# Second head's z in seven block products, with the fourth block sum made earlier

## The chip, the core and the metric

The kernel runs on one core of one Trainium2 chip. The metric is the device time of one execution in microseconds (us), median of several runs. The profile shows the core's engines: TensorE (PE, matmuls; PEld its weight loads), VectorE (DVE), ScalarE (ACT), GpSimd (POOL), and the queue of SyncE (SP), which issues most DMAs.

## What is computed

A decoder trunk of two layers over x of 1024 tokens by 1024 channels in float32: a gated DeltaNet layer (GDN), then an mLSTM layer, then a norm. The change is in the GDN layer alone:

```
h = rmsnorm(x, norm_w[i])
p = h @ w_in                                  # q, k, v, z, a, bt of 8 heads
q, k, v = silu(causal_dwconv(qkv))            # q, k: 128 wide a head, v: 256
q, k = l2norm(q) * HEAD_QK ** -0.5, l2norm(k)
# per head, by chunks: S_t = exp(g_t)(I - beta_t k_t k_t^T) S_{t-1} + beta_t k_t v_t^T;  o_t = S_t^T q_t
o = gated_delta_chunked(q, k, v, g, beta)
o = rmsnorm(o, norm_w) * silu(z)
x = x + o @ w_out
```

z of a head is 256 columns of h @ w_in.

## The kernel before

**Precision.** Each operand of the large products is split in a high and a low part (`hi` and `lo`, L280 on ScalarE and L281 on GpSimd or, for some, VectorE), and each product takes three matmuls: hi by hi, hi by lo, lo by hi.

**Blocks.** h is cut in four blocks A11, A12, A21, A22 (first index the half of the tokens, second the half of the channels). From them come the sums S1 to S4, made once for the whole layer: S1 = A21 + A22, S3 = A21 - A11, S2 = S1 - A11 by `h_blocks` (L486, L488, L489 on VectorE, split by L468 on ScalarE and L469), four channel blocks one after the other; S4 = A12 - S2 by `last_block` (L473, L477, L478 on VectorE, split by L468 and L469). S4 is put where A21's tiles were. A pair of column blocks of the weights can then be multiplied in two ways. `Columns` takes the blocks as they are: eight products. `Pair` takes seven (in the manner of Strassen and Winograd) and needs S1 to S4, sums of weights (L596, L597, L603, L604) and sums of results (L626, L631, L637, L643, L651, all on VectorE), and seven split operands where `Columns` splits four. One product (`product`, L511) is twelve matmuls of 128x512. In before heads 0 and 1 have their z by `Columns`, all later heads by `Pair`.

**Order.** TensorE's order is written by hand. Three matmuls of `product` are a step; `plan` names for each step the generators that run a bit there: `gdn_scan` (the chunks of a head's scan), `gdn_keys`, `gdn_queries`, `gdn_solve`, `gdn_merge`, `gdn_tokens`, `first_blocks`, `last_block`. The numbers are in the tables KEYS, QUERIES, SOLVE, MERGE, TOKENS, SCAN (one entry each for head 0, head 1 and all later heads, counted from the head's base), BLOCKS and LAST. A base is the number of steps of the heads before: 64 for the first, 96 for the second, 88 for each later one. A scheduler sets the order on the other engines from the order in which the code runs and from its estimates, so that a table's number moves instructions there too.

**The scan.** A chunk c of head h is `ks` (TensorE, state by key, L1061), `rr` (VectorE, L1063), `y` (TensorE, L1066), `w` (ScalarE, L1068), `sn` and `o` (TensorE, L1073, L1082, L1083), the new state S (VectorE, L1078; L1076 for the first chunk), then the gate and its transposes `go` (L386, L383). Each waits for the one ahead. Chunks are numbered 0 to 7: y0_7 is the last `y` of head 0. While head 0 is scanned, head 1's columns are multiplied (gkv1, gvq1, gz1, named `gkv_ps`, `gvq_ps`, `gzp_ps` in the trace), its keys prepared (`tpk` L886, `kk` L928, `nt` L931, two halves: kk1_0 and kk1_1), its triangular system solved on VectorE (L977, L979, 31 rounds) and merged (`xp`, `yl`, L1016; the solution goes through DRAM as `tb` and comes back as `td`, copied by L1006 and transposed by L1002).

Of the kernel before, what the change touches and what calls it, by code (L numbers as in the profile page):

```python
# [17 lines left out]
P = 128  # L18
# [23 lines left out]
OUT0 = "k", "wraw"  # L42
VT = ("ccpx", "ccpb")

F0STEPS = 6, 16
R8 = range(8)
LOOK = 2
VLO = (((1, 3, 6, 7), (1, 2, 3, 5, 7)), ((3, 6, 7), (1, 3, 5, 7)))
# [6 lines left out]
LASTENDS = ((4, 4), (6, 8), (8, 8))  # L55


KEYS = ((4, 9, 10, 17), (26, 29, 30, 33), (22, 25, 26, 29))
QUERIES = ((20, 22, 25, 32), (68, 71, 76, 76), (80, 80, 84, 89))
SOLVE = (24, 41, 38)  # L60
MERGE = (78, 97, 89)
TOKENS = ((37, 37, 81, 85), (74, 77, 100, 106), (64, 74, 103, 109))
SCAN = (95, 110, 102)
PACE = ((3, 3, 8), (4, 3, 10), (4, 3, 11))
BLOCKS = (106, 115, 114, 126)
XLOADS = (24, 116)
LAST = (158, 148, 156, 164)
TH = HT * P


# [1 line left out]
def hybrid_kernel(ctx, tc, x_in, norm_w, final_norm_w, gdn_w_in, gdn_conv_w, gdn_a_log, gdn_dt_bias, gdn_norm_w,  # L72
# [422 lines left out]
    def last_block(temp, e):  # L495

        for k in range(4):
            a = temp(k)
            whole(V, a, blocks["A12"][k])
            add_parts(V, a, a, blocks["S2"][k], ALU.subtract)  # L500
            put("S4", k, a, e)
            yield
# [202 lines left out]
    def out_heads(half, heads, gs, name):  # L705

        for jj in range(0, KT // 2, 2):
            pss = [pwork(f"{name}{half}_{jj}{i}", "ppbx"[i]) for i in range(4)]
            for h in heads:
                for j in range(2):  # L710
                    hi, lo = operand()
                    for i in range(2):
                        for e in range(ET):
                            ghi, glo = gs[h, e]
                            for m, (a, b) in enumerate(((hi, ghi), (hi, glo), (lo, ghi))):
                                mm(pss[2 * j + i], a[:, e, i * P:(i + 1) * P], b, start=h == heads[0] and e == 0 and m == 0,  # L716
                                   stop=h == heads[-1] and e == ET - 1 and m == 2)
                            if (i, e) != (1, ET - 1):
                                yield
                    if h == heads[-1]:  # L720
                        for i in range(2 * j, 2 * j + 2):
                            V.tensor_tensor(x[2 * jj + i][half], x[2 * jj + i][half], pss[i], ALU.add)
                    yield
# [27 lines left out]
    def do(gen, n=1):  # L751
        for _ in range(n):
            next(gen, None)
# [100 lines left out]
    def gdn_z(h, st):  # L854
        st["gate"] = [None, None]

        def sink(e, half, src):
            if st["gate"][half] is None:
                st["gate"][half] = hp.tile([P, ET, TH], F32, tag="gate", bufs=GB, name=f"gz{h}_{half}")
            A.activation(st["gate"][half][:, e, :], src, AF.Silu)  # L860

        c0 = 2 * QK + DI + h * DV
        if h < 2:
            return Columns(gdn_w_in, c0, c0 + P, f"gzp{h}", sink, small=h == 0)
        return Pair(gdn_w_in, c0, c0 + P, f"gzp{h}", sink, in_psum=(True, False), bank="b")

    def gdn_tokens(h, st):

        for half in range(2):
            v = hp.tile([P, HT, DV], F32, tag="v", bufs=2, name=f"gv{h}_h{half}")  # L870
            st["v"].append(v)
            for e in range(ET):
                vp = pwork(f"gvp{h}_{e}_{half}", "d")
                for c in range(HT):
                    nc.tensor.transpose(vp[:, c * P:(c + 1) * P], st["vt"][e, half][:, c * P:(c + 1) * P], ident)
                A.copy(v[:, :, e * P:(e + 1) * P], vp.rearrange("p (c d) -> p c d", c=HT))
                if e == ET - 1:
                    G.tensor_tensor(v, v, st["irk"][:, half * HT:half * HT + HT].unsqueeze(2).to_broadcast([P, HT, DV]),
                                    ALU.mult)
                yield  # L880
# [62 lines left out]
    def gdn_queries(h, st):  # L943

        sq, eq = (sp.tile([P, NT], F32, tag=n, name=f"{n}{h}") for n in ("sq", "eq"))
        st["eq"] = eq
        for half in range(2):
            hs = slice(half * HT, half * HT + HT)
            q, k, at = st["q"][half], st["k"][half], st["at"][half]
            squares_t(q, sq, "q", h, half)  # L950
            V.tensor_scalar(eq[:, hs], sq[:, hs], 1e-6, EPS * DK, ALU.add, ALU.mult)
            dec_b = decay_row(1, h, half)
            yield
            kq = pwork(f"kq{h}_{half}", "d").rearrange("p (c i) -> p c i", c=HT)
            for c in range(HT):
                s_ = slice(c * P, (c + 1) * P)
                mm(kq[:, c, :], k[:, s_], q[:, s_], start=True, stop=True)
            V.tensor_tensor(at, kq, at, ALU.mult)
            G.tensor_tensor(q, q, dec_b, ALU.mult)
            yield  # L960

    def gdn_solve(h, st):


        nd = st["nd"].rearrange("p (j i) -> p j i", i=BLK)
        rows = sp.tile([P, BLK // NG4 * BLK], F32, tag="t", bufs=2, name=f"xr{h}")
        nc.sync.dma_start(rows, unit_rows)
        xp = pwork(f"xt{h}", "x")[:, :BLK // NG4 * BLK] if h > 1 else rows
        xt = xp.rearrange("p (i r) -> p i r", r=BLK)
        if h > 1:  # L970
            A.copy(xp, rows)
        yield
        for j in range(BLK - 1):
            m, n = j // NG4 + 1, BLK - 1 - j
            pr = sp.tile([P, m, n], F32, tag="td", bufs=1, name=f"pr{h}_{j}")
            with behind() if j == 0 else nullcontext():
                V.tensor_tensor(pr, xt[:, :m, j:j + 1].to_broadcast([P, m, n]),  # L977
                                nd[:, j:j + 1, j + 1:].to_broadcast([P, m, n]), ALU.mult)
            st["solved"] = V.tensor_tensor(xt[:, :m, j + 1:], xt[:, :m, j + 1:], pr, ALU.add)  # L979
            yield  # L980
        st["tb"] = dp.tile([NG4, NT, NB, BLK // NG4, BLK], F32, tag="tb", bufs=2, name=f"tb_dram{h}")
        if h > 1:
            A.copy(rows, xp)
        nc.sync.dma_start(st["tb"].rearrange("g c b i r -> (g c b) (i r)"), rows)
        st["td"] = tds = sp.tile([P, NT, BLK], F32, tag="td", bufs=1, name=f"td{h}")
        for g in range(NG4):
            nc.sync.dma_start(tds[g::NG4], st["tb"][g].rearrange("c b i r -> (b i) c r"))
        yield
# [124 lines left out]
    with tc.manual_schedule(engines={mybir.EngineType.PE}):  # L1113
        sts = [{} for _ in range(H)]
        diags = []
        cols = [c for h in range(H) for c in (*gdn_columns(h, sts[h]), gdn_z(h, sts[h]))]
        gs = [{}, {}]
        parts0 = g_parts(gg_dram, range(H - 1), 0, gg_place(0), "gl", gs[0])
# [21 lines left out]
        def at_steps(steps, gen):  # L1140
            for step in steps:
                plan.setdefault(step, []).append(gen)

        base, starts = 0, []
        for h in range(H):
            starts.append(base)
            base += (64, 96)[h] if h < 2 else 88
        end = base
        for h, (st, base) in enumerate(zip(sts, starts)):
            i = min(h, 2)  # L1150
            b, (l, m, p) = SCAN[i] + base, PACE[i]
            scan = [b, b + m]
            for c in range(1, NT):
                c0 = b + m + p - l - m + p * (c - 1)
# [3 lines left out]
        for h, (st, base) in enumerate(zip(sts, starts)):  # L1158
            i = min(h, 2)
            off = lambda steps: [base + n for n in steps]  # L1160
            at_steps(off(range(MERGE[i] - 4, MERGE[i] + 16, 4)), gdn_merge(h, st))
            at_steps(off(KEYS[i]), gdn_keys(h, st, range(2)))
            at_steps(off(QUERIES[i]), gdn_queries(h, st))
            at_steps(off(SOLVE[i] + n // 2 for n in range(BLK + 1)), gdn_solve(h, st))
            at_steps(off(TOKENS[i]), gdn_tokens(h, st))
        temps = lambda k: [wp.tile([P, TH], F32, tag="wraw", bufs=WB, name=f"hs{k}_{i}") for i in range(2)]

        def first_blocks():
            gen = h_blocks(temps, (G, V, G))
            for k in range(4):  # L1170
                with tc.issue_after(sts[0]["merged" if k else "solved"].ins):
                    next(gen)
                yield

        at_steps(BLOCKS, first_blocks())
        at_steps(LAST, last_block(lambda k: temps(k)[0], V))

# [430 lines left out]
    with tc.manual_schedule(engines={mybir.EngineType.PE}):  # L1608
# [5 lines left out]
        for n, _ in enumerate(out_heads(1, heads, gss[1], "lout")):  # L1614
            if n == F0STEPS[0]:
                do(f0)
            if n >= F0STEPS[1] and n % 2 == 0:
                do(f0)
# [61 lines left out]
```

## Time and profile before

| | us |
|---|---|
| median of three runs | 1923.8 (1923.57 to 1925.78) |
| the profiled execution | 1924.86 |
| its span | 1923.1 |
| TensorE busy | 1872.0 (97%), 9764 matmuls |
| VectorE busy | 1256.2 (65%) |
| ScalarE busy | 1016.1 (53%) |
| GpSimd busy | 701.4 (36%) |

The page gives the busy time of each engine, the span in slices, and the costliest groups. Matmuls overlap, so their busy times add up to more than the time they take; the distance from one start to the next is what one costs. The list of waits gives, for an engine, who ended its idle time; the timeline gives single instructions with start, duration and, in brackets, the idle time ahead of them.

### The profile page before, as it was taken

What the parts mean: (1) busy time and instruction counts of PE and PEld (TensorE: products, weight loads), DVE (VectorE), ACT (ScalarE), POOL (GpSimd) and SP (SyncE); (2) the same over time, 40 slices, a digit from 0 to 9 for tenths busy, and PEclk for the clock granted to TensorE, in tenths of its full rate; (3) what the DMA queues carried; (4) which work ended last, traced back from release to release, by engine and by line L of the source; (5) the groups of instructions that cost most, each with busy time, mean ns of one, the idle gap of its engine ahead of it and who ended that gap; (6) DMA issues with size and microseconds to landing.
All of it is one profiled execution on the core that took longest, in us unless ns stands there. A gap on an engine that the chain in (4) does not pass through costs nothing. (4 is left out here: it accounts for less than half of the span.)

```text
span 1923.1 us, 28886 instructions
## 1 busy us (share of the span) xinstructions
PE 1872.0 (97%) x9764; PEld 1545.2 (80%) x9764; DVE 1256.2 (65%) x2856; ACT 1016.1 (53%) x2336; POOL 701.4 (36%) x662
## 2 busy tenths in 40 slices
PE   5999999999999999999999999999999999999998
PEld 3777888888888887788878888888888888878886
DVE  7579686859585858548566866666666666673413
ACT  5555565655556555545346454555454555574523
POOL 4234334343433434101031433333333333345553
PEclk9999999999999999999999999999999999999999
DMA  4211122222222222646322221212121222245342
GB/s 144 92 48 55 48 72 80 62 77 66 68 78 64 79 59 90 198 130 215 121 71 73 66 77 56 79 58 83 61 83 61 72 69 66 77 140 181 131 137 72
DMA packets 138621, 171.25 MB, mean 89 GB/s; under 512 B 30860, under 2 KB 68584, under 8 KB 138472
## 3 DMA queue, kind: packets, MB, share of 16 engines
q1 hardware_dynamic: 137896, 168.87, 28.0%
q8 instruction: 77, 1.26, 0.3%
q14 instruction: 72, 0.59, 0.1%
q10 hardware_dynamic: 576, 0.52, 0.1%
HBM read 142.87 MB, written 26.48 MB: 88 GB/s over the span
## 5 line engine op out<-in xcount | busy, mean ns | idle before, releaser
L425 POOL TENSOR_TENSOR g_r<-g_r,mhalf 128x1 f32<-128x1 f32 x64 | 40.3, 629 | 195.3 <-DVE g_r L424 194.6
L286 DVE SCALAR_TENSOR_TENSOR gw_lo<-gw_raw,rest,gw_hi 128x256 fp32r<-128x256 f32 x128 | 64.1, 539 | 63.8 <-ACT gw_hi L285 63.6
L281 POOL TENSOR_TENSOR lw_lo<-lw_raw,lw_hi 128x512 fp32r<-128x512 f32 x56 | 72.4, 1296 | 73.8 <-ACT lw_hi L280 67.9
L281 POOL TENSOR_TENSOR mz_lo<-mz_raw,mz_hi 128x512 fp32r<-128x512 f32 x40 | 53.7, 1342 | 102.9 <-ACT mz_hi L280 102.7
L285 ACT ACTIVATE gw_hi<-gw_raw,rest 128x256 fp32r<-128x256 f32 x128 | 58.0, 501 | 61.8 <-PE gout L716 34.1
L716 PE MATMUL lout<-lgp_hh,lw_hi 128*128 128x512 f32 x224 | 88.6, 395 | 0.9 <-DVE mg L1371 0.9
L281 POOL TENSOR_TENSOR mog_lo<-mog_raw,mog_hi 128x512 fp32r<-128x512 f32 x39 | 51.4, 1319 | 104.1 <-ACT mog_hi L280 104.1
L716 PE MATMUL lout<-lgp_hh,lw_lo 128*128 128x512 f32 x224 | 87.3, 390 | 0.0
L716 PE MATMUL lout<-lgp_hl,lw_hi 128*128 128x512 f32 x224 | 87.2, 389 | 0.0
L281 POOL TENSOR_TENSOR mv_lo<-mv_raw,mv_hi 128x512 fp32r<-128x512 f32 x38 | 51.9, 1366 | 83.2 <-ACT mv_hi L280 50.6
L511 PE MATMUL gkv_ps<-hh,gkv_hi 128*128 128x512 f32 x176 | 77.6, 441 | 0.0
L280 ACT CAST lw_hi<-lw_raw 128x512 fp32r<-128x512 f32 x56 | 34.6, 620 | 79.2 <-PE lout L716 41.1
L281 POOL TENSOR_TENSOR gzp_lo<-gzp_raw,gzp_hi 128x512 fp32r<-128x512 f32 x38 | 50.0, 1317 | 67.6 <-ACT gzp_hi L280 53.9
L281 POOL TENSOR_TENSOR gkv_lo<-gkv_raw,gkv_hi 128x512 fp32r<-128x512 f32 x40 | 52.2, 1304 | 61.6 <-ACT gkv_hi L280 56.0
L281 POOL TENSOR_TENSOR mkq_lo<-mkq_raw,mkq_hi 128x512 fp32r<-128x512 f32 x35 | 45.1, 1289 | 75.2 <-ACT mkq_hi L280 61.8
L511 PE MATMUL gkv_ps<-hh,gkv_lo 128*128 128x512 f32 x176 | 69.4, 394 | 0.0
L511 PE MATMUL gkv_ps<-hl,gkv_hi 128*128 128x512 f32 x176 | 69.0, 392 | 0.0
L716 PE MATMUL gout<-glp_hh,gw_hi 128*128 128x512 f32 x160 | 66.5, 415 | 0.0
L425 POOL TENSOR_TENSOR m_r<-m_r,mhalf 128x1 f32<-128x1 f32 x64 | 42.9, 671 | 59.4 <-DVE m_r L424 52.6
L281 POOL TENSOR_TENSOR gqv_lo<-gqv_raw,gqv_hi 128x512 fp32r<-128x512 f32 x30 | 40.4, 1345 | 64.1 <-PE sn L1073 27.1
L716 PE MATMUL gout<-glp_hh,gw_lo 128*128 128x512 f32 x160 | 62.7, 392 | 0.0
L716 PE MATMUL gout<-glp_hl,gw_hi 128*128 128x512 f32 x160 | 62.4, 390 | 0.0
(765 smaller groups left out, 6653.2 us busy)
## 6 DMA issues: line engine op xcount, KB each, us to landing
gw_raw<-in_gdn_w_out_dram SPq DMA_DIRECT2D x64, 256.0 KB, 2.8
lw_raw<-in_mlstm_w_out_dram SPq DMA_DIRECT2D x56, 256.0 KB, 2.8
gzp_raw<-in_gdn_w_in_dram SPq DMA_DIRECT2D x32, 256.0 KB, 3.2
growb<-g_dram SPq DMA_DIRECT2D x32, 256.0 KB, 3.3
gg_dram<-gv_h SPq DMA_DIRECT2D x64, 128.0 KB, 1.8
gl<-gg_dram SPq DMA_DIRECT2D x32, 256.0 KB, 3.4
mog_raw<-in_mlstm_w_in_dram SPq DMA_DIRECT2D x32, 256.0 KB, 3.1
mz_raw<-in_mlstm_w_in_dram SPq DMA_DIRECT2D x32, 256.0 KB, 3.0
```

The source lines that it names most:

```text
L280: A.copy(hi, raw)
L281: (e or G).tensor_tensor(lo, raw, hi.bitcast(F32), ALU.subtract)
L285: A.activation(hi[:, k], raw[:, k], AF.Copy, scale=c)
L286: V.scalar_tensor_tensor(lo[:, k], raw[:, k], c, hi.bitcast(F32)[:, k], ALU.mult, ALU.subtract)
L425: G.tensor_tensor(r, r, mhalf[:, :1], ALU.pow)
L511: mm(ps, w_[:, k, :], h_, start=first and k == 0 and i == 0, stop=k == 3 and i == 2, skip_group_check=True)
L716: mm(pss[2 * j + i], a[:, e, i * P:(i + 1) * P], b, start=h == heads[0] and e == 0 and m == 0, stop=h == heads[-1] and e == ET - 1 and m == 2)
```

## The change

Head 1's z becomes a `Pair`, as the later heads' is, and only head 0 keeps `Columns`. Its 32 steps become 28, so the second head's length is 92 and all later bases are four sooner. S4 must now be there for head 1's z (steps 148 to 151) and not first for head 2: LAST goes from steps 148 to 164 to steps 123 to 142. BLOCKS, the scan of head 0 (two steps sooner), the second half of head 1's keys (three later), its queries and solve (four later), and the queries and solve of the later heads get other steps.

```diff
-KEYS = ((4, 9, 10, 17), (26, 29, 30, 33), (22, 25, 26, 29))
-QUERIES = ((20, 22, 25, 32), (68, 71, 76, 76), (80, 80, 84, 89))
-SOLVE = (24, 41, 38)
+KEYS = ((4, 9, 10, 17), (26, 29, 30, 36), (22, 25, 26, 29))
+QUERIES = ((20, 22, 25, 32), (72, 75, 80, 80), (78, 78, 83, 87))
+SOLVE = (32, 45, 29)
...
-SCAN = (95, 110, 102)
+SCAN = (93, 110, 102)
...
-BLOCKS = (106, 115, 114, 126)
+BLOCKS = (98, 119, 111, 123)
...
-LAST = (158, 148, 156, 164)
+LAST = (123, 130, 136, 142)
...
         c0 = 2 * QK + DI + h * DV
-        if h < 2:
-            return Columns(gdn_w_in, c0, c0 + P, f"gzp{h}", sink, small=h == 0)
+        if h == 0:
+            return Columns(gdn_w_in, c0, c0 + P, f"gzp{h}", sink, small=True)
         return Pair(gdn_w_in, c0, c0 + P, f"gzp{h}", sink, in_psum=(True, False), bank="b")
...
-            base += (64, 96)[h] if h < 2 else 88
+            base += (64, 92)[h] if h < 2 else 88
```

On TensorE, in the second head's first stretch of gvq1, there stands before, from the second half of the keys (kk1_1) over the first chunk's `sn` and `o`:

```order
L928 MATMUL kk1_1_1521<-gkT1_1_1280 128x128 x4
L511 MATMUL gvq1_ps00_1504<-hh0_2_0_243,gvq1_00_hi_1295 128x512
L511 MATMUL gvq1_ps00_1504<-hl0_2_0_244,gvq1_00_hi_1295 128x512
L511 MATMUL gvq1_ps00_1504<-hh0_2_0_243,gvq1_00_lo_1296 128x512
L1073 MATMUL sn0_0_1543<-w0_0_1502,kd0_668 128x256
L1083 MATMUL o0_0_1547<-w0_0_1502,at0_0_682 128x256
```

and a little further on, from `ks` of chunk 1, in after:

```order
L1061 MATMUL ks0_1_1531<-S0_0_1515,gkT0_0_368 128x256
L511 MATMUL gvq1_ps00_1504<-hh0_3_0_248,gvq1_00_hi_1295 128x512
L511 MATMUL gvq1_ps00_1504<-hl0_3_0_249,gvq1_00_hi_1295 128x512
L511 MATMUL gvq1_ps00_1504<-hh0_3_0_248,gvq1_00_lo_1296 128x512
L511 MATMUL gvq1_ps01_1505<-hh0_0_1_408,gvq1_00_hi_1295 128x512
L511 MATMUL gvq1_ps01_1505<-hl0_0_1_409,gvq1_00_hi_1295 128x512
L511 MATMUL gvq1_ps01_1505<-hh0_0_1_408,gvq1_00_lo_1296 128x512
L928 MATMUL kk1_1_1563<-gkT1_1_1280 128x128 x4
```

So kk1_1 stood ahead of `sn` and `o` of chunk 0 and now stands behind `ks` of chunk 1.

On VectorE at the same place (L931 is nt of the keys' first half, L486 to L489 and L469 the block sums, L326 a convolution) there stands before:

```order
L931 SCALAR_TENSOR_TENSOR nt1_0_1454<-kk1_0_1449,nb1_1404,at1_0_1420 128x128 x4
L326 SCALAR_TENSOR_TENSOR gvT1_0_1_1493<-gkv1_ps11_1288,gcw_159,gvT1_0_1_1493 128x511
L486 TENSOR_TENSOR hs2_1_1790<-x2_1_80,x6_1_88 128x512
L469 TENSOR_TENSOR S2hl1_1777<-hs1_1_1764,S2hh1_1776 128x512
L910 TENSOR_TENSOR kd1_1406<-tpk1_1_1471,ekd_277 128x512
L920 TENSOR_SCALAR sk1_1401<-sk1_1401 128x4
L326 SCALAR_TENSOR_TENSOR gvT1_0_1_1493<-gkv1_ps11_1288,gcw_159,gvT1_0_1_1493 128x510
L488 TENSOR_TENSOR hs2_0_1789<-x2_1_80,x2_0_79 128x512
L1076 COPY S0_0_1545<-sn0_0_1543 128x256
```

and now:

```order
L931 SCALAR_TENSOR_TENSOR nt1_0_1458<-kk1_0_1453,nb1_1404,at1_0_1420 128x128 x4
L486 TENSOR_TENSOR hs2_1_1810<-x2_1_80,x6_1_88 128x512
L1076 COPY S0_0_1515<-sn0_0_1513 128x256
L326 SCALAR_TENSOR_TENSOR gvT1_0_1_1497<-gkv1_ps11_1288,gcw_159,gvT1_0_1_1497 128x511
L469 TENSOR_TENSOR S2hl1_1696<-hs1_1_1683,S2hh1_1695 128x512
L910 TENSOR_TENSOR kd1_1406<-tpk1_1_1475,ekd_277 128x512
```

The first state S0_0, which ks0_1 needs, comes six rows nearer to L931.

On VectorE at the end of head 0's scan (rr0_7 is what y0_7 needs; S4hl, hs and the S2 tiles belong to S4) there stands before:

```order
L1063 SCALAR_TENSOR_TENSOR rr0_7_2167<-ks0_7_2165,nlam_276,gv0_h1_1305 128x256
L1002 STREAM_TRANSPOSE nd1_1405<-td1_1868 32x8x32 x3
L469 TENSOR_TENSOR S4hl0_2175<-hs0_0_2169,S4hh0_2174 128x512
L469 TENSOR_TENSOR S4hl1_2231<-hs1_0_2225,S4hh1_2230 128x512
L473 TENSOR_TENSOR hs2_0_2252<-hh0_6_0_263,hl0_6_0_264 128x512
L473 TENSOR_TENSOR hs3_0_2318<-hh0_7_0_268,hl0_7_0_269 128x512
L477 TENSOR_TENSOR hs2_0_2252<-hs2_0_2252,S2hh2_1802 128x512
```

and now:

```order
L977 TENSOR_TENSOR pr1_28_1896<-xr1_1652,nd1_1405 128x24
L1063 SCALAR_TENSOR_TENSOR rr0_7_2206<-ks0_7_2204,nlam_276,gv0_h1_1305 128x256
L979 TENSOR_TENSOR xr1_1652<-xr1_1652,pr1_28_1896 128x8x3
L637 TENSOR_TENSOR gzp1_u4_2113<-gzp1_u4_2113,gzp1_ps7_2152 128x512
L977 TENSOR_TENSOR pr1_29_1928<-xr1_1652,nd1_1405 128x16
L979 TENSOR_TENSOR xr1_1652<-xr1_1652,pr1_29_1928 128x8x2
L977 TENSOR_TENSOR pr1_30_1931<-xr1_1652,nd1_1405 128x8
L979 TENSOR_TENSOR xr1_1652<-xr1_1652,pr1_30_1931 128x8
L643 TENSOR_TENSOR gzp1_ps5_2114<-gzp1_u2_1961,gzp1_ps5_2114 128x512
```

S4's work stands ahead of rr0_7 now, and the end of the second head's solve (L977, L979) has come behind it.

## Rows read from the trace of the kernel before

**Rows 1.** The page, first part: busy time, share of the span and instructions.

```profile
PE 1872.0 (97%) x9764; PEld 1545.2 (80%) x9764; DVE 1256.2 (65%) x2856; ACT 1016.1 (53%) x2336; POOL 701.4 (36%) x662
```

**Rows 2.** Windows: length, then busy us (instructions) of each engine, clock, DMA.

```profile
140.00:180.00 40.00, 35.44 (x171) 28.35 (x170) 36.00 (x72) 22.52 (x59) 19.52 (x16) 0.96 0.17 50
```

**Rows 3.** Waits of TensorE, 140 to 260 us: total, times, longest.

```profile
PE kk L928 <- DVE nt L931: 2.8, 1, 2.8
PE y L1066 <- DVE rr L1063: 0.9, 1, 0.9
PE ks L1061 <- DVE S L1078: 0.4, 1, 0.4
PE yl L1016 <- ACT nd L1033: 0.4, 1, 0.4
PE gvp L875 <- ACT sqrq L889: 0.3, 1, 0.3
```

**Rows 4.** Timeline, TensorE: start, duration, instruction, [idle before it and its releaser].

```profile
145.79 1.05 PE L928 MATMUL kk<-gkT 128*128 128x128 f32 x8
...
153.35 1.53 PE L928 MATMUL kk<-gkT 128*128 128x128 f32 x8 [2.85 <-DVE nt L931]
...
215.03 0.59 PE L1066 MATMUL y<-rr,nt 128*128 128x256 f32 x2
...
223.88 0.69 PE L1016 MATMUL xp<-nd,nt 32*32 32x32 f32 x32
```

**Rows 5.** Windows, TensorE alone: length, busy (instructions), granted clock, DMA.

```profile
153.97:157.39 3.42, 3.42 (x13) 0.50 0.58 173
```

**Rows 6.** Timeline, VectorE, from 143.5 us to rr0_7.

```profile
143.70 0.42 DVE L1037 COPY nt<-yl 64x256 f32<-64x256 f32 x1 [6.16 <-ACT nt L1036]
144.04 1.18 DVE L486 TENSOR_TENSOR hs<-x,x 128x512 f32<-128x512 f32 x1
...
152.17 1.13 DVE L931 SCALAR_TENSOR_TENSOR nt<-kk,nb,at 128x128 f32<-128x128 f32 x4
...
195.38 0.17 DVE L951 TENSOR_SCALAR eq<-sq 128x4 f32<-128x4 f32 x1 [0.45 <-ACT sqrq L889]
...
210.26 0.48 DVE L1078 SCALAR_TENSOR_TENSOR S<-S,dec,sn 128x256 f32<-128x256 f32 x1 [3.96 <-PE sn L1073]
211.34 0.42 DVE L386 TENSOR_TENSOR gv_h<-go_gp,gz 128x256 f32<-128x256 f32 x1 [0.60 <-PE go_gp L383]
...
213.17 0.48 DVE L1063 SCALAR_TENSOR_TENSOR rr<-ks,nlam,gv_h 128x256 f32<-128x256 f32 x1 [1.25 <-PE ks L1061]
```

**Rows 7.** Timeline, TensorE in head 0's z: two matmuls twelve starts apart.

```profile
104.82 0.39 PE L511 MATMUL gzp_ps<-hh,gzp_lo 128*128 128x512 f32 x1
...
107.54 0.39 PE L511 MATMUL gzp_ps<-hh,gzp_lo 128*128 128x512 f32 x1
```

**Rows 8.** Timeline, VectorE and (one row) GpSimd, 168 to 173 us.

```profile
168.08 0.68 DVE L469 TENSOR_TENSOR S2hl<-hs,S2hh 128x512 fp32r<-128x512 f32 x1
168.68 0.68 DVE L473 TENSOR_TENSOR hs<-hh,hl 128x512 f32<-128x512 f32 x1
...
170.41 1.74 DVE L477 TENSOR_TENSOR hs<-hs,S2hh 128x512 f32<-128x512 f32 x1
...
170.32 1.28 POOL L281 TENSOR_TENSOR gzp_lo<-gzp_raw,gzp_hi 128x512 fp32r<-128x512 f32 x1 [1.15 <-ACT gzp_hi L280]
```

**Rows 9.** Timeline, SyncE's queue, GpSimd and VectorE: the solve's way through DRAM.

```profile
202.96 0.42 SPq L984 DMA_DIRECT2D tb_dram<-xr  x1
...
209.06 1.26 POOL L1006 COPY nt<-td 32x128 f32<-32x128 f32 x4 [0.33 <-DMA td<-tb_dram]
...
213.57 1.32 DVE L1002 STREAM_TRANSPOSE nd<-td 32x256 f32<-32x256 f32 x3
```

**Rows 10.** Waits of TensorE, 740 to 800 us (the last head's queries).

```profile
PE kq L957 <- ACT sqrq L889: 0.7, 1, 0.7
PE go_gp L383 <- DVE at L958: 0.5, 1, 0.5
```

More of the change, by code (lines that the diff above doesn't have):

```diff
@@ L43 @@
 VT = ("ccpx", "ccpb")
-F0STEPS = 6, 16
+F0STEPS = (6, 16)
 R8 = range(8)
```

## The prediction, made before the changed kernel was run

> **What bounds the kernel now.** The page's first part comes first: TensorE is busy 97% of the span [rows 1], so a gain is either matmul time taken out or one of the few stretches in which TensorE waits. Next the table by stretch: from 140 to 180 us TensorE is busy only 35.44 of 40 us, while VectorE has its fullest stretch, 36.00 of 40 [rows 2]. This is where the first head's scan, the second head's keys and the sums of blocks of h run together. The list of waits says for whom TensorE waits there: 2.8 us for kk1_1, 0.9 for y0_2, 0.4 for ks0_3, all on VectorE, and 0.4 for yl on ScalarE [rows 3]. The timeline places the longest at 153.35 [rows 4]. Behind it the granted clock is 0.50 (1.2 GHz) for 3.42 us, which did some 1.7 us of work at the full level [rows 5]. VectorE's own timeline shows why: after 143.70 it has no idle time at all until 195.38, so in these 52 us it is the bound and TensorE waits on what stands late in its row [rows 6]. Behind that it idles 0.45 + 3.96 + 0.60 + 1.25 = 6.26 us before rr0_7 [rows 6], the last thing that the first head's scan needs of it (y0_7, at 215.03 [rows 4]).
>
> **Part 1: twelve matmuls fewer.** The second head's z is 7 products of 12 matmuls in place of 8. Each shows 0.39 us of busy time, but they overlap: twelve take 107.54 - 104.82 = 2.72 us from start to start [rows 7], 0.227 each. Everything behind z is four steps of three matmuls sooner: -2.7 us. Nothing hides this; it is TensorE time. A saving by busy time (12 x 0.39 = 4.7) would count the overlap twice. (The Trainium skill, "TensorE: Matmul & The Clock Gate", section "Back-to-back issue gap", gives about 131 ns for a sustained N=512 matmul and about 216 ns for an isolated one; by these twelve would be estimated at 1.6 or 2.6 us. The trace is nearer the second, and its own 0.227 goes into the sum.)
>
> **Part 2: what the seventh product costs elsewhere.** The pair needs 7 split operands, not 4, and sums around them. On VectorE eight instructions of 128x512 come before rr0_7 (L596, L597, L603, L604, two L281, L626, L631); three more (L637, L643, L651) come behind. S4 moves about 20 steps forward: in before its ten instructions (L473, L477, L478 for two blocks, L469 for four) ran from 214.92 on, behind rr0_7; in after the order puts them ahead. So 18 instructions are new before rr0_7. One shows 0.68 us but the next starts 0.60 later [rows 8]: 18 x 0.60 = +10.8 us. Some five small steps of the solve move behind rr0_7 (0.85 us less). One copy of y's operand ScalarE makes 0.4 sooner, since in after the exp of at1_1 stands behind it: 0.4 sooner start, and one hold of 0.5 at 144.04 [rows 6] avoided.
>
> Where does 10.8 us go? In before the stretch from 143.70 to rr0_7's end, 213.65, holds 69.95 - 6.26 = 63.7 us of service [rows 6]. In after it starts at 143.3 and needs 63.7 + 10.8 - 0.85 - 0.5 = 73.15: rr0_7 ends no sooner than 216.45 if VectorE never idles and is held as often as before. TensorE, on the other side, would be there without any wait at 215.03 - 1.37 (y0_7 is two steps sooner in the order) - (0.37 + 2.85 + 1.7 + 0.95 + 0.40 + 0.30 of waits [rows 3] and half clock) = 207.1. VectorE is 9 us later, so **VectorE bounds the whole stretch**, and which wait the new order removes is then of no worth: the time is made up at the next one.
>
> Holds. Of the 63.7 us some 12 are 15 instructions that last longer than their kind because a GpSimd instruction is under way: the L477 at 170.41 takes 1.74 us against 0.68, with GpSimd's subtraction at 170.32 lasting 1.28 [rows 8]. The first is the L486 at 144.04, 1.18 us long [rows 6]. That is 0.8 us each, and nearly each 128x512 instruction of GpSimd holds one. In after GpSimd has one more (five of gz1's splits, not four), and three that fell into VectorE's idle time (the copies at 209.06 [rows 9] and one on either side) now meet work: 4 x 0.8 = 3.3 us at most, none if they meet the instructions that read PSUM. At anchors VectorE may idle for TensorE's chain as before, 0 to 3.5 us. I take 1.6 for both, nearer the low ends, since a bound engine's own idle is small in rows 6 up to 195: rr0_7 ends at 218.0, y0_7 at 218.05 against 215.03 - 1.37 = 213.67 at the same step of before: **+4.4 us** (range -1 to +8; it falls below nothing if holds fall by a third).
>
> (The Trainium skill, "SBUF — State Buffer", section "Who interferes with whom", speaks against this change: VectorE and GpSimd share a port pair as an exclusive lock, a VectorE instruction with two SBUF inputs contends with a GpSimd instruction that reads SBUF, and whichever is second waits for the whole of the other. The trace agrees: 170.32 + 1.28 + 0.60 is the end of that L477. By it S4's ten and most of the pair's adds are of the kind that is held, which is the second rival.)
>
> **Part 3: the moved waits.** kk1_1 goes from step 98 to 101 and comes behind ks0_1 (order, TensorE). Its wait on L931 (152.17 + 1.13 [rows 6]) goes. But ks0_1 now needs S0_0, and that copy (L1076) stands right behind L931 and one L486 in VectorE's row: 153.3 + 0.6 + 0.4 - 0.4 to 0.9 = 153.4 to 153.9. TensorE is at ks0_1, from kk1_0 at 145.79 [rows 4] and what stands between, at about 151.5. So a wait of some 2 us on S0_0 takes the place of the 2.85 on L931; whether the clock halves behind it changes little, because VectorE's total sets y0_7. This is inside the +4.4.
>
> **Part 4: what comes right behind.** The second head's solve ends behind rr0_7, about 1.6 us after its end. In before it goes to DRAM at 202.96 and its copies from there start at 209.06 and take 1.26 us, L1002's transposes 1.32 [rows 9]: 7.4 us at the least from the solve's end to xp1's operand, 8.7 if the two stand one behind the other, so 9.0 to 10.3 behind rr0_7. TensorE has xp1 at 223.88, 8.85 us behind y0_7 [rows 4], and two steps more lie between them in after: 10.2. The slack, some 13 us in before, is 0 to 1 us. I take +0.2 (0 to 2). tpk2_1 comes four steps sooner and waits on VectorE as its kind does in later heads: +0.3 (0.2 to 1.0). For heads 2 to 6 the order of all engines is the same but for a place or two: 0. In the last head kq waits 0.7 on sqrq and go_gp 0.5 on `at` [rows 10]; in after both stand ahead of the weights' casts: -0.7 (-1.2 to 0).
>
> **The sum.** -2.7 + 4.4 + 0.2 + 0.3 - 0.7 = +1.5 us on the profiled execution's 1924.86: 1926.4. That execution lies 1.1 us over the median of the three runs; the median goes from 1923.8 to about **1925.2**. A measurement of this kernel can tell 0.2%, 3.85 us, from no change, so this is no change that can be told: below 1919.95 is faster, above 1927.65 slower.
>
> **Rivals.** (a) *VectorE has room after all*: holds fall since other instructions meet GpSimd's, and the waits vanish. With all gone y0_7 is at 207.1: -6.6 - 2.7 - 0.7 = -10 us, 1914. It is faster by the bound as soon as rr0_7 ends before about 212.7, 3.7 us under my floor: five holds fewer out of 15. For it: the 18 new instructions are placed by a scheduler where it sees gaps, and 6.26 us of idle time are there to be filled. Against: that idle time is counted in already. Half way it gives 1917 to 1919.9. Chance 0.17. (b) *GpSimd holds VectorE for most of the added work* (other side, slower): four GpSimd instructions more that each hold one (+3.3), idle at anchors of 2.5, so rr0_7 ends at 222.2 and xp1 waits 1 us on top: +8.6 - 2.7 + 1 + 0.3 - 0.3 = +6.9, 1930.7. It decides from rr0_7's end at 220.4 on, five holds over my floor. Chance 0.25, centre 1929, since its parts need not all come. (c) *The change doesn't do what it says*: S4 sooner and other places move only waits that VectorE's total sets anyway, and only the twelve matmuls count if VectorE's added work went entirely into idle time: 1923.8 - 2.7 - 0.4 = 1920.7. This is inside my forecast's bound of no change, with a part of its chance.
>
> **How the numbers follow.** No change 0.58 (around 1925.2, from 1920 to 1927.6 by the ends of parts 2 and 4), faster 0.17, slower 0.25. To leave out no more than 2 in 10 the range takes in half way into (a) and most of (b): 1918 to 1930.
>
> **What would show it.** Right: 9752 matmuls; no wait of kk1_1 on L931 but one of about 2 us of ks0_1 on L1076 near 153.5; VectorE without idle time from 143.3 to rr0_7; further waits of TensorE on L1063 and L1078 at several of y0_2 to y0_7, 9 to 12 us in all from 140 to 220; y0_7 near 218; S4's rows near 165 to 205. Wrong if VectorE idles more than 3 us in that stretch (then the order, not its service, is the bound), if the long L477 and L473 are gone (a), if xp1 waits over 1 us (b), or if time moves outside 140 to 260 us, above all in heads 2 to 6, where I put nothing.

## The result and the profile after

The changed kernel takes 1928.2 us in the median of 12 runs (1926.22 to 1934.05), the kernel before 1924.72 beside it (12 runs): ratio 1.0024, 95% interval 1.0016 to 1.0031. That is 3.5 us slower by the medians and 4.6 by the ratio, on either side of the 0.2% that was taken as the bound of no change. Eleven further runs of the same changed kernel, below, gave 1.0014 (1.0005 to 1.0023), just inside it. Single runs scatter by several us, so the sums below are made in the traces, stretch by stretch.

The page of the changed kernel, first part:

```profile
PE 1869.7 (97%) x9752; PEld 1543.6 (80%) x9752; DVE 1264.4 (66%) x2867; ACT 1015.4 (53%) x2340; POOL 702.2 (36%) x663
```

Twelve matmuls are gone, and the eleven VectorE instructions of the pair have come. Two windows (columns as in [rows 2]):

```profile
140.00:180.00 40.00, 35.47 (x172) 28.70 (x171) 35.53 (x73) 24.14 (x61) 19.59 (x16) 0.96 0.17 50
180.00:220.00 40.00, 36.96 (x185) 31.04 (x184) 36.56 (x105) 19.54 (x54) 15.96 (x14) 1.00 0.17 56
```

From 140 to 180 us nothing is gained. The second of the two stood in before as

```profile
180.00:220.00 40.00, 39.70 (x197) 33.15 (x196) 32.24 (x96) 19.61 (x56) 14.85 (x17) 1.00 0.20 63
```

TensorE was busy 39.70 us there and is busy 36.96 now, VectorE 36.56 in place of 32.24: the second half of head 0's scan has become as full on VectorE as the first.

Waits of TensorE, 50 to 260 us (total, times, longest), which answer to [rows 3]:

```profile
PE kq L957 <- DVE gv_h L386: 3.0, 1, 3.0
PE ks L1061 <- DVE S L1076: 2.8, 1, 2.8
...
PE ks L1061 <- DVE S L1078: 1.2, 1, 1.2
PE tpk L886 <- DVE kd L910: 0.8, 1, 0.8
PE y L1066 <- DVE rr L1063: 0.6, 1, 0.6
```

The wait of kk1_1 on L931 is gone, and ks0_1 waits 2.8 us on S0_0 (L1076) in its place. A second, which nobody had in before, is 3.0 us of kq1_1 on a gate (L386). TensorE's timeline shows their places (it answers to [rows 4]):

```profile
154.50 0.70 PE L1061 MATMUL ks<-S,gkT 128*128 128x256 f32 x2 [2.77 <-DVE S L1076]
...
211.37 0.82 PE L957 MATMUL kq<-gqT,gkT 128*128 128x128 f32 x5 [3.04 <-DVE gv_h L386]
...
216.26 0.59 PE L1066 MATMUL y<-rr,nt 128*128 128x256 f32 x2
```

and VectorE's the two ends of the stretch (it answers to [rows 6]):

```profile
143.40 0.42 DVE L1037 COPY nt<-yl 64x256 f32<-64x256 f32 x1 [5.75 <-ACT nt L1036]
...
214.77 0.48 DVE L1063 SCALAR_TENSOR_TENSOR rr<-ks,nlam,gv_h 128x256 f32<-128x256 f32 x1
```

VectorE's row from 143.40 to rr0_7 has some 2.6 us of idle time, the smallest gaps counted, against 8.0 in before by the same count, and none ahead of rr0_7 itself, which waited 1.25 there before. y0_7 stands at 216.26, without a wait and 1.0 us behind rr0_7's end (215.25): the last large wait ahead of it is kq1_1's. The same step of before was at 213.67. So the stretch gave back 2.6 of the 2.7 us that the twelve matmuls save.

Where the rest goes shows when the two traces are laid side by side at fixed points of TensorE's order (starts, us):

| point or stretch | before | after | difference |
|---|---|---|---|
| kk1_0 (step 94) | 145.79 | 145.89 | +0.1 |
| y0_7 | 215.03 | 216.26 | +1.2 (two steps sooner in the order) |
| kk1_0 to kk7_0 (keys of the last head) | 556.86 | 556.84 | 0.0 |
| kk7_0 to y7_0 | 82.20 | 85.47 | +3.3 |
| y7_0 to the mLSTM layer's gates | 220.56 | 221.79 | +1.2 |
| from there to the end | 911.44 | 912.16 | +0.7 |

From kk1_0 to the last head's keys the changed kernel is even. It loses in the last head, 3.3 us, which is the place where I had a gain of 0.7. Waits of TensorE from 760 to 800 us in the changed kernel (they answer to [rows 10]):

```profile
PE yp L1016 <- ACT nd L1021: 2.1, 1, 2.1
PE yp L1016 <- DVE nd L1022: 0.4, 1, 0.4
PE kq L957 <- DVE gv_h L386: 0.3, 1, 0.3
PE xp L1016 <- ACT sqrq L889: 0.2, 1, 0.2
```

The wait on `at` is gone and that on sqrq is down to 0.2 us, as was said. But yp, a product of the last head's merge, waits 2.1 us on ScalarE's copy nd (L1021), and behind that wait the granted clock falls (windows, TensorE alone, columns as in [rows 5]; 0.76 over 7.2 us is some 3.5 us at the lower level, 1.2 GHz, which costs 1.7):

```profile
774.80:782.00 7.20, 6.75 (x69) 0.76 0.67 197
```

2.1 + 0.4 + 1.7 of new loss, less the 0.5 + 0.7 of [rows 10], is +3.0 of the 3.3. Why the copy is late shows on the timelines of ScalarE, VectorE and SyncE's queue; in the changed kernel:

```profile
766.20 0.90 ACT L285 ACTIVATE gw_hi<-gw_raw,rest 128x256 fp32r<-128x256 f32 x2
...
766.79 1.92 DVE L286 SCALAR_TENSOR_TENSOR gw_lo<-gw_raw,rest,gw_hi 128x256 fp32r<-128x256 f32 x2 [1.02 <-POOL g_r L425]
...
768.74 0.81 SPq L733 DMA_DIRECT2D gw_raw<-in_gdn_w_out_dram  x2
...
773.51 0.91 ACT L285 ACTIVATE gw_hi<-gw_raw,rest 128x256 fp32r<-128x256 f32 x2 [5.01 <-DMA gw_raw<-in_gdn_w_out_dram]
774.44 0.36 ACT L1021 COPY nd<-xp 32x256 f32<-32x256 f32 x1
```

and the like rows of the kernel before:

```profile
763.69 0.91 ACT L285 ACTIVATE gw_hi<-gw_raw,rest 128x256 fp32r<-128x256 f32 x2 [3.68 <-DMA gw_raw<-in_gdn_w_out_dram]
...
766.25 0.38 SPq L733 DMA_DIRECT2D gw_raw<-in_gdn_w_out_dram  x1
...
770.45 0.91 ACT L285 ACTIVATE gw_hi<-gw_raw,rest 128x256 fp32r<-128x256 f32 x2 [0.67 <-DMA gw_raw<-in_gdn_w_out_dram]
771.38 0.36 ACT L1021 COPY nd<-xp 32x256 f32<-32x256 f32 x1
```

ScalarE makes the last head's sqrq ahead of the cast of an output weight (gw_hi, L285). The cast comes 2.5 us later (766.20 against 763.69), VectorE's second half of it (L286) frees the buffer later, the next weight's load is issued 2.5 us later (768.74 against 766.25), and the next cast, which waits for it, stands ahead of the copy nd in ScalarE's row: 774.44 against 771.38.

### The profile page after: what moved, and what is told of

It reads as the page before. It is cut to its first block, busy times and chain, and to the rows that moved or that the text cites. A ratio compares the mean times of both kernels' runs of the same rounds, so it can differ in the third digit from the quotient of the medians.

```text
span 1928.4 us, 28877 instructions
## 1 busy us (share of the span) xinstructions
PE 1869.7 (97%) x9752; PEld 1543.6 (80%) x9752; DVE 1264.4 (66%) x2867; ACT 1015.4 (53%) x2340; POOL 702.2 (36%) x663
## 5 line engine op out<-in xcount | busy, mean ns | idle before, releaser
L286 DVE SCALAR_TENSOR_TENSOR gw_lo<-gw_raw,rest,gw_hi 128x256 fp32r<-128x256 f32 x128 | 60.6, 511 | 66.0 <-ACT gw_hi L285 64.8
L285 ACT ACTIVATE gw_hi<-gw_raw,rest 128x256 fp32r<-128x256 f32 x128 | 57.9, 500 | 58.1 <-PE gout L716 32.1
L281 POOL TENSOR_TENSOR mv_lo<-mv_raw,mv_hi 128x512 fp32r<-128x512 f32 x38 | 50.3, 1324 | 82.2 <-ACT mv_hi L280 53.2
```

Source lines behind the costliest of these rows:

```text
L281: (e or G).tensor_tensor(lo, raw, hi.bitcast(F32), ALU.subtract)
L285: A.activation(hi[:, k], raw[:, k], AF.Copy, scale=c)
L286: V.scalar_tensor_tensor(lo[:, k], raw[:, k], c, hi.bitcast(F32)[:, k], ALU.mult, ALU.subtract)
```

## The experiments

Two theories after the result. **A**: the loss comes from the later heads' entry of QUERIES by way of the weights' loads; the second head's pair is worth nothing either way. **B**: the pair and its work on VectorE is the loss, and the last head is chance. For the pair itself, **C**: VectorE's work sets the end of the scan, so the pair pays back what it saves; against **D**: the order or TensorE's chain sets it. Each ratio is against the kernel before, of 11 runs (10 for kq_sooner and blocks_v) unless said otherwise. "Scan" is the time from y0_0 to y0_7, read in one trace of each kernel: 70.80 us in the changed kernel's.

**again**: the changed kernel, unaltered.

> The changed kernel once more, unaltered, to see which of its lost time repeats from one profiled execution to the next. Theory A (last head): from 705 to 809 us it loses some 3 us against before (a wait of yp on ScalarE's nd of about 2.1 us and half clock behind it); ratio about 1.002. Rival B (chance): the wait at yp is absent in this execution and the loss is spread elsewhere.

Ratio 1.0014 (1.0005 to 1.0023). Scan 70.78. The waits up to 705 us are the same to 0.3 us, one by one. The wait of yp is there again, ScalarE held by the same load, but shorter (lists of waits, TensorE and ScalarE):

```profile
PE yp L1016 <- ACT nd L1021: 1.1, 1, 1.1
...
ACT gw_hi L285 <- DMA gw_raw<-in_gdn_w_out_dram: 4.0, 1, 4.0
```

and the clock is 1.00 over the whole stretch (window):

```profile
760.00:800.00 40.00, 37.84 (x270) 30.17 (x269) 25.86 (x53) 24.16 (x62) 8.32 (x11) 1.00 0.66 200
```

So the last head loses 0.6 us here and 3.3 there. The wait repeats, its price does not. The 1.0 us between the two waits is that of the weight's load: from its issue to the cast it takes 4.8 us in the first trace (768.74 to 773.51) and 3.8 here (770.19 to 773.96).

**q2_old**: the later heads' QUERIES as in before.

```diff
-QUERIES = ((20, 22, 25, 32), (72, 75, 80, 80), (78, 78, 83, 87))
+QUERIES = ((20, 22, 25, 32), (72, 75, 80, 80), (80, 80, 84, 89))
```

> The changed kernel with only the later heads' entry of QUERIES set back to that of before (80, 80, 84, 89). Theory A (the earlier queries of the last head put ScalarE's casts of the output weights, and so the loads behind them, later): no wait at yp, 3 us less than the changed kernel, ratio to before 1.0000 to 1.0008. Rival B (the loss comes from the second head's pair): 0 us against the changed kernel, ratio 1.0018 to 1.0025. What I had predicted of the last head (a gain of 0.7 by the new entry) would make it slower by 0.7: 1.0028.

0.9996 (0.9987 to 1.0004), 3.5 us less than the unaltered kernel beside it on the same chip. The yp wait is not there; from the last head's keys to y7_0 it takes 80.1 us, against 85.5 and 82.8 with the new entry and 82.2 in before. Over all traces of this document that stretch takes 80.0 to 82.2 us in the ten with the old entry and 82.8 to 85.5 in the four with the new one. A holds, and with this one entry put back the changed kernel is even with the one before. Its own scan is 72.1 us, although its instructions on TensorE and VectorE stand in the changed kernel's order up to there: behind kq1_1's wait its clock falls (last section). Most runs below are built on q2_old, so their scans are held against two traces, 70.8 and 72.1, and a difference of about 1.3 us can be the clock alone.

**b_q2_new**: the kernel before with that entry alone.

```diff
-QUERIES = ((20, 22, 25, 32), (68, 71, 76, 76), (80, 80, 84, 89))
+QUERIES = ((20, 22, 25, 32), (68, 71, 76, 76), (78, 78, 83, 87))
```

> The kernel before with only the later heads' entry of QUERIES changed to that of the changed kernel (78, 78, 83, 87). Theory A: the whole loss of the last head shows here, +3 us, ratio 1.0013 to 1.0020, and from 705 to 809 us the same yp wait. Rival B: 0. As predicted: -0.7 us, 0.9996.

1.0010 (1.0001 to 1.0019): +1.9 us, a little under what A said, and its interval takes in 3. The yp wait comes with the entry, without any pair (TensorE's timeline, ScalarE's list of waits, and the window):

```profile
774.50 0.21 PE L1016 MATMUL yp<-nd,nt 32*32 32x32 f32 x1 [1.25 <-ACT nd L1021]
...
ACT gw_hi L285 <- DMA gw_raw<-in_gdn_w_out_dram: 4.1, 1, 4.1
...
760.00:800.00 40.00, 37.73 (x262) 29.94 (x261) 24.94 (x53) 22.86 (x60) 7.39 (x10) 0.96 0.62 190
```

So A is shown from both sides: taken away it takes the loss with it, put in alone it brings it.

**z1_cols**: the pair undone, all else as in q2_old.

```diff
-        if h == 0:
-            return Columns(gdn_w_in, c0, c0 + P, f"gzp{h}", sink, small=True)
+        if h < 2:
+            return Columns(gdn_w_in, c0, c0 + P, f"gzp{h}", sink, small=h == 0)
...
-            base += (64, 92)[h] if h < 2 else 88
+            base += (64, 96)[h] if h < 2 else 88
```

> The changed kernel with the later heads' QUERIES as before and the second head's z in eight products again (96 steps), all other numbers as changed, S4 still made early. Eight VectorE instructions of 0.60 us less ahead of rr0_7, twelve matmuls more behind. Theory C: from kk1_0 to y0_7 some 3 us less, behind it 2.7 us more: within 1 us of the kernel with the pair, ratio to before 0.999 to 1.001. Rival D (VectorE's added work costs nothing): 2.7 us slower than with the pair, ratio 1.0010 to 1.0014.

0.9998 (0.9989 to 1.0007), against 0.9996 with the pair: no difference. Scan 68.3, that is 2.5 us less than in the changed kernel (3.8 less than in q2_old), and 2.7 us of matmuls more behind it. VectorE has idle time again ahead of the last S and rr, 11.1 us in the whole stretch to rr0_7 against 2.6 (VectorE's timeline, with one row of ScalarE):

```profile
206.59 0.48 DVE L1078 SCALAR_TENSOR_TENSOR S<-S,dec,sn 128x256 f32<-128x256 f32 x1 [2.58 <-PE sn L1073]
...
211.17 0.48 DVE L1063 SCALAR_TENSOR_TENSOR rr<-ks,nlam,gv_h 128x256 f32<-128x256 f32 x1 [0.75 <-PE ks L1061]
...
212.56 1.31 ACT L468 CAST S4hh<-hs 128x512 fp32r<-128x512 f32 x2 [1.17 <-PE gzp_ps L511]
...
213.22 1.39 DVE L469 TENSOR_TENSOR S4hl<-hs,S4hh 128x512 fp32r<-128x512 f32 x2 [0.33 <-ACT S4hh L468]
```

This is near C's number, but not by C's count. The expectation says that S4 is still made early, and the last two rows show that it isn't: S4 is put where A21's tiles were, the eight products of z still read A21, S4's first cast waits for one of them (gzp_ps), and S4's ten instructions come behind rr0_7, as in before. So all 18 new instructions are gone from the stretch, 10.8 us of VectorE's work, and not eight with 4.8. What the run shows is the pair together with the early S4 that it asks for: what it saves on TensorE, the two give back on VectorE. How much of the 2.5 to 3.8 us is the pair's own isn't shown.

**s4_light**: S4 without S2 (the expectation says what is left out).

```diff
             whole(V, a, blocks["A12"][k])
-            add_parts(V, a, a, blocks["S2"][k], ALU.subtract)
             put("S4", k, a, e)
```

> The changed kernel with S4 made without subtracting S2: eight VectorE instructions of 128x512 (L477, L478 of four blocks, 0.60 us each) are left out of the GDN layer, all ahead of rr0_7; the rest of the order stays nearly as it is. Theory C (VectorE's total work sets the end of the first head's scan): y0_7 comes 4 to 5 us sooner than the changed kernel's 216.3, at 211 to 212, and the whole is 4 us shorter than the changed kernel, ratio to before about 1.0000. Rival D (the chain of the scan or the order sets it): y0_7 within 1 us of 216.3, whole within 1 us of the changed kernel.

1.0012 (1.0003 to 1.0021). Scan 69.65: 1.1 us less, where C had said 4 to 5. The eight instructions are gone, but the scheduler filled the room: the last round of the second head's solve starts at 211.29 in place of 217.35 (timeline; line numbers are one higher in this kernel), while kq1_1 still waits 2.7 us for VectorE:

```profile
211.29 0.17 DVE L980 TENSOR_TENSOR xr<-xr,pr 128x8 f32<-128x8 f32 x1
...
215.90 0.59 PE L1067 MATMUL y<-rr,nt 128*128 128x256 f32 x2
```

So C in its plain form falls: it isn't VectorE's total alone that counts but what stands ahead of the scan's S, rr and gates in its row. The solve, which is needed later, is put between them.

**kq_sooner**: kq1_1 ahead of the gate on which it waits (on q2_old).

```diff
-QUERIES = ((20, 22, 25, 32), (72, 75, 80, 80), (80, 80, 84, 89))
+QUERIES = ((20, 22, 25, 32), (72, 75, 77, 78), (80, 80, 84, 89))
```

> The changed kernel with the later heads' QUERIES as before, and the second head's last two QUERIES steps from 80 to 77 and 78, so that kq1_1 stands ahead of the gate's transposes go0_5 on TensorE and no longer behind them. Theory C (VectorE's row sets the end of the first head's scan): the 3 us wait of kq1_1 on L386 goes, but rr0_7 stands where it stood and y0_7 gets a wait in its place; from kk1_0 to y0_7 at most 1.5 us less, ratio to before 0.999 to 1.000. Rival E (the wait is one of a result bank that the transposes hold, and VectorE has room): from kk1_0 to y0_7 3 us less, ratio 0.998.

1.0002 (0.9992 to 1.0011). The 3 us wait is gone, and ks0_7 has one of 2 us on VectorE's S0_6 nearly at the same time (TensorE's timeline):

```profile
211.97 0.70 PE L1061 MATMUL ks<-S,gkT 128*128 128x256 f32 x2 [2.05 <-DVE S L1078]
```

Scan 70.39, 0.4 less than the changed kernel and 1.7 less than q2_old, whose clock falls behind the wait of kq1_1; here it stays at 1.00 behind the 2 us. Two thirds of the wait taken away came back at the next meeting point, where VectorE's row was still late.

**scan95**: the first head's scan two steps later, as in before (on q2_old).

```diff
-SCAN = (93, 110, 102)
+SCAN = (95, 110, 102)
```

> The changed kernel with the later heads' QUERIES as before and the first head's scan two steps later again (95). Theory C: VectorE's row sets the end, TensorE's place matters little: the wait of ks0_1 on S0_0 shrinks by about 1.4 us, y0_7 comes at the same time within 1 us. Rival (the order of TensorE sets it): y0_7 1.4 us later and the whole 1.4 us slower.

1.0010 (1.0001 to 1.0019), 2.7 us more than q2_old in the median of ratios. From kk1_0 to y0_7 it takes 71.9, against 70.4 in the changed kernel and 71.7 in q2_old, and the wait on S0_0 grows to 3.6 us (TensorE's timeline):

```profile
157.00 0.70 PE L1061 MATMUL ks<-S,gkT 128*128 128x256 f32 x2 [3.59 <-DVE S L1076]
```

My expectation failed: VectorE's order follows the code's, so a scan asked for later also gets its copies later on VectorE. The copy of S0_0 starts 4.3 us behind L931 here and 1.6 us behind it in the changed kernel. Against the changed kernel's trace, where the clock stays up at the end as it does here, the two steps of the change bring 1.5 us; against q2_old's own it is 0.2. The intervals of the two ratios overlap, so that they bring anything in the whole isn't shown.

**blocks_v**: subtractions of S1 and S3 on VectorE (on q2_old).

```diff
-            gen = h_blocks(temps, (G, V, G))
+            gen = h_blocks(temps, (V, V, V))
```

> The changed kernel with the later heads' QUERIES as before and the subtractions of S1 and S3 on VectorE instead of GpSimd: eight GpSimd instructions of 1.28 us less, eight VectorE instructions of 0.60 more, six of them between kk1_0 and rr0_7. Theory H (each such GpSimd instruction holds one of VectorE for 0.8 us): VectorE gains 6 x (0.8 - 0.6) = 1.2 us, from kk1_0 to y0_7 1 us less, and the wait of ks0_1 on S0_0 is shorter. Rival (holds cost nothing where VectorE has other work): 6 x 0.6 = 3.6 us more to y0_7, ratio to before 1.001 to 1.002.

1.0002 (0.9993 to 1.0011): no difference in the whole. Scan 70.06, 0.7 less than in the changed kernel and 2.0 less than in q2_old (in both q2_old and this run the clock falls behind kq1_1's wait of 3.1 us, which stays), though VectorE does 3.6 us more work of its own there. The wait on S0_0 is gone; part of it comes back as smaller ones, of which the largest is this (TensorE's timeline):

```profile
175.18 0.67 PE L1066 MATMUL y<-rr,nt 128*128 128x256 f32 x2 [1.90 <-DVE rr L1063]
```

The holds can be counted. In q2_old 15 GpSimd instructions of 128x512 fall into the stretch up to rr0_7, and 13 of VectorE's are long, by 11.0 us together; here they are 9 and 9, by 6.4 us. Six of VectorE's own instructions more and 4.7 us of holds less: theory H stands, at nearly 0.8 us for each of the six.

**k1_early**, **kall_early**: one or all of the three held-back channel blocks of S1 to S3 let go before the merge (on q2_old; kall_early has `sts[0]["solved"]` alone).

```diff
-                with tc.issue_after(sts[0]["merged" if k else "solved"].ins):
+                with tc.issue_after(sts[0]["merged" if k > 1 else "solved"].ins):
```

> The changed kernel with the later heads' QUERIES as before, and the second of the four channel blocks of S1 to S3 no longer held back until the first head's merge is done: the order puts its four VectorE instructions of 0.60 us ahead of L1037, into idle time of VectorE before 143.4 us. No work is added or left out. Theory C (VectorE's work between kk1_0 and rr0_7 sets the end of the scan): 2.4 us of work and some holds of 0.8 leave the stretch, from kk1_0 to y0_7 2 to 3.5 us less than 70.4, ratio to before 0.998 to 0.999. Rival (the order refills what is freed, as it did where S4 was made lighter): at most 1 us less, ratio 0.9994 to 1.000.

> The same with all four channel blocks let go early: twelve VectorE instructions, 7.2 us, come ahead of L1037, more than the idle time of 5.8 us there holds. Theory C: from kk1_0 to y0_7 5 to 7 us less than 70.4, the wait of ks0_1 on S0_0 gone, but yl or y0_0 waits 1 to 3 us for VectorE's copies; ratio 0.997 to 0.999. Rival (order refills): 0.9995 to 1.000, or slower by the waits at the merge.

1.0015 (1.0006 to 1.0024) and 1.0040 (1.0026 to 1.0053, 5 runs). The idle time of 5.75 us ahead of L1037 was not free: the copies and products around the merge wait behind the added work, and in k1_early TensorE's clock is low behind it (timeline and window):

```profile
139.37 0.33 PE L875 MATMUL gvp<-ident,gvT 128*128 128x128 f32 x1 [2.53 <-ACT gv_h L876]
...
140.00:180.00 40.00, 36.91 (x178) 29.89 (x177) 29.26 (x63) 22.98 (x57) 17.08 (x13) 0.87 0.17 47
```

In kall_early the merge's own product waits longest (TensorE's timeline):

```profile
137.30 0.21 PE L1016 MATMUL yp<-nd,nt 32*32 32x32 f32 x1 [2.86 <-ACT nd L1022]
```

kk1_0 comes at 152.2 and 156.6 in place of 145.9. In kall_early the scan's stretch is shorter by 3.3 us from kk1_0 on; in k1_early it isn't (70.71). What was said of the stretch holds half in kall_early and not in k1_early. The price ahead of it was put at 1 to 3 us for kall_early and is 11; k1_early, for which none was put, pays 6.

**combo**, **combo_all**: kq_sooner, blocks_v and the early block or blocks together.

> The second channel block early, the subtractions of S1 and S3 on VectorE, and kq1_1 ahead of go0_5, with the later heads' QUERIES as before: the three changes that each shortened or should shorten the stretch, together. Theory C: from kk1_0 to y0_7 4 to 5 us less than 70.4, ratio to before 0.997 to 0.998, better than both kernels. Rival: the gains do not add, ratio 0.999 to 1.000.

> The same with all four channel blocks early. Theory C: from kk1_0 to y0_7 6 to 8 us less than 70.4, paid back in part by 1 to 3 us of waits at the first head's merge; ratio 0.996 to 0.998. Rival: the merge's waits eat it, ratio 0.999 to 1.001.

0.9996 (0.9987 to 1.0005) and 1.0010 (1.0001 to 1.0019). In combo the scan is down to 66.9 us, 3.9 less than in the changed kernel, but kk1_0 ahead of it comes 3 us later. In combo_all it takes 67.7 us from kk1_0 to y0_7, 2.7 less where 6 to 8 were expected, and kk1_0 comes 7 us later. No version measured here beats the kernel before by what can be told.

## Why the prediction was right where it was, and where not

The median was put at 1925.2 with a range of 1918 to 1930, no change the likeliest and slower at 0.25. It came to 1928.2, at the edge between the two. The sum was +1.5 on the profiled execution and the traces show +5.3; by its terms:

- **Part 1**, -2.7: right. 9752 matmuls, and behind the scan's end all is four steps sooner.
- **Part 2**, +4.4: right in that VectorE's row bounds the stretch, too large; y0_7 is +2.6 late at its step, and TensorE's waits from 140 to 220 us add up to 7.6 us, not 9 to 12. rr0_7 ended at 215.25, not 218.0. The term of the sum that was mis-sized is the 1.6 for holds and idle time. 13 instructions are long, by 11.0 us, where before has 15 with 12.2 (counted where one lasts 0.25 us more than its kind), so none of the four further holds showed; VectorE's idle time was 2.6 us. The floor of 216.45 was undercut by 1.2 as well. It took holds as fixed and 63.7 us as service; the row of before is not quite without gaps from 143.70 to 195.38, and with the smallest ones it idles 8.0 us and not 6.26. Nor did rr0_7 set y0_7, which came 1.0 us behind its end. What the pair costs by itself no run shows: z1_cols takes it out together with the early S4, 2.5 to 3.8 us.
- **Part 3**, a wait of about 2 us of ks0_1 on S0_0: it is 2.77, with 3.4 us at half clock behind it. That the half clock changes little, as was said, is shown: in q2_old the wait is 2.79 and the clock stays at 1.00, and y0_6 stands 57.25 us behind kk1_0 there and 57.35 in the changed kernel. Not foreseen was the place of the next large one, kq1_1 on L386, the last ahead of y0_7.
- **Part 4**, xp1 +0.2: no wait was seen. tpk2_1 +0.3: 0.82 us against 0.21, +0.6. Heads 2 to 6, 0: right. **The last head, -0.7: the step that failed.** I read from the order that sqrq and `at` now stand ahead of the weights' casts, priced the two waits that this removes, and did not follow the casts: the loads queued behind their buffers, and the copy queued behind the next cast on ScalarE. It is +3.3 in this trace, +0.6, +1.3 and +2.4 in the three others with the new entry, and the two runs that take the entry out or put it in alone give 3.5 and 1.9 us.

Rival (b), slower, had its time nearly right (1929 to 1930.7) for a reason that the traces do not show: neither more holds nor a wait of xp1. That the median stayed inside the range is therefore luck in part: part 2 was put too high, and the last head, booked as a gain, lost. With its entry put back (q2_old) the kernel stands at 0.9996, 0.8 us below before and even with it by the interval, where the sum without its last term says 2.2 above. Rivals (a) and (c) are out: VectorE had no room, and of the 2.7 us that the matmuls save the stretch gave back 2.6. What is left, some 1 to 2 us between y7_0 and the end in the profiled execution, stays open; the same stretches vary by as much among the other traces, so I put it to no cause.

## What to carry over

Work that left the full engine for one that is also full in that stretch was worth nothing here, however long that engine's slack is elsewhere: lay the helper's row of the stretch beside the main engine's and compare where each would be alone. An instruction that is moved ahead of a cast or split also moves the buffer's release, the load that waits for it and all that stands behind the next cast: follow that chain once round before a wait is booked as saved. A run that takes one thing out may take out more: look in its trace for what was to stay before its time is read (z1_cols). And idle time ahead of a serial step (here the merge) is part of that step; filling it lengthened the step by more than was put in.

## What the runs showed of the hardware

The granted clock does not follow the length of a wait alone. In the changed kernel the waits of 2.77 us (ks0_1) and 2.13 us (yp) are followed by a stretch at the lower level, the one of 3.04 us (kq1_1) is not. In q2_old, whose TensorE and VectorE have the same instructions in the same order up to here, it is the other way round: the clock stays up behind ks0_1's 2.79 us and falls behind kq1_1's 3.05 (windows, TensorE alone, two of the changed kernel, then two of q2_old):

```profile
154.50:160.00 5.50, 5.50 (x22) 0.69 0.42 129
211.40:217.00 5.60, 5.60 (x29) 1.00 0.47 142
...
152.80:158.30 5.50, 5.48 (x28) 1.00 0.46 129
209.60:215.20 5.60, 5.60 (x22) 0.73 0.40 138
```

The fall behind kq1_1 shows in the time: from y0_6 to y0_7 it takes 13.0 us in the changed kernel and 14.4 in q2_old. In the unaltered repeat the yp wait of 1.1 us leaves the clock at 1.00, and with b_q2_new one of 1.25 is followed by 0.96 over 40 us. So the same wait can cost about 1.5 us more in one execution than in the next. What decides it was not tried.
